# Retention heads summed ungated, and the first gate's rows weighed on VectorE

## The chip, the cores and the metric

The kernel runs on one core of one Trainium2 chip. The time is the device time of one execution in microseconds; smaller is better. The core's engines named below are PE (TensorE, matrix products), DVE (VectorE), ACT (ScalarE), POOL (GpSimd) and SP (SyncE, which here does nothing but issue transfers). The kernel before has three timed runs: 1186.47, 1186.53 and 1189.27 us, so a median of 1186.53 us.

## The reference, cut to what matters

The model is a two-layer diffusion transformer on 256 latent tokens `x` and 256 context tokens `ctx`, each of width 1024, in fp32. Layer 1 mixes tokens by retention (four heads, 256-wide queries and keys, 512-wide values), layer 2 by neighbourhood attention; each layer ends in an MLP with 4096 hidden units. Shifts, scales and gates come from a conditioning vector, through a 1024 x 6144 matrix per layer, once for the latent and once for the context tokens.

```python
for i in range(DEPTH):
    mod = (silu_c @ ada_w[i] + ada_b[i])[:, None, :]
    mod_c = silu_cc @ ada_w[i] + ada_b[i]
    sh1, sc1, g1, sh2, sc2, g2 = jnp.split(mod, 6, axis=-1)
    sh1c, sc1c, g1c, sh2c, sc2c, g2c = jnp.split(mod_c, 6, axis=-1)
    h = x * (1.0 + sc1) + sh1
    hc = ctx * (1.0 + sc1c) + sh1c
    ...                                   # y, yc: the mixer's outputs
    x = layer_norm(DN_ALPHA * x + g1 * y, ln_g[i, 0], ln_b[i, 0])
    h = x * (1.0 + sc2) + sh2
    x = layer_norm(DN_ALPHA * x + g2 * sq_relu_mlp(h, mlp_w1[i], mlp_w2[i]), ...)
    ...                                   # the same for ctx in layer 1
# retention, end of the mixer: heads side by side, then one product
on = on.transpose(0, 2, 1, 3).reshape(b, o.shape[2], v_w)
return (on * jax.nn.silu(g)) @ w_o
```

So the retention's output y is a sum over four heads of a (512-wide) product with that head's rows of `w_o`. The gate `g1` multiplies this sum column by column, and `DN_ALPHA * x` is added to it before the LayerNorm.

## The kernel before, in words

**Products.** Every large product is made of three passes (`mm3`): each operand is split into a rounded high part and the rest, and hi·hi, hi·lo and lo·hi are added in PSUM. Weights come in pieces of 512 KB: SP issues the load into one of four `raw` buffers, ACT casts it to `hi`, and DVE subtracts to make `lo`. The transposed, modulated input (`hTh`, `hTl`) of all 512 tokens stays in SBUF. `R[t]`, t = 0 to 3, holds the residual of the 128-token tile t (two of `x`, two of `ctx`).

**Retention heads.** The loop `for h in range(RH)` does four heads. In each, PE makes queries and keys (tiles `pq`, rotated by DVE and ACT), values (`pv`, evacuated to `vh`, `vl`), the scores (`pS`, which DVE masks with `strips` into `sm` and splits into `sh`, `sl`), the silu gates of tiles 0 and 1 (`pg`), the heads' outputs (`po`, one bank per tile), the gates of tiles 2 and 3, and the output product `pw` with eight 128 x 512 blocks (four tiles, two halves). DVE normalises each `po` as soon as it is done (`bn_stats` into `bs`, `bn_aggr` into `mv`, then `on`, with a `rstd` worked out on POOL), and POOL multiplies it with the silu gate into `gs`. PE transposes `gs` (`pT`) between the products of the gates of tiles 2 and 3 and, for tiles 2 and 3, between the first `pw` blocks; ACT and DVE split that into `oh` and `ol`, the left operand of `pw`.

**The residual.** In the first head ACT multiplies `R` by `ALPHA`. In every head `tok` hands each `pw` block to `accumulate`: DVE makes `acc = pw * G1`, and POOL adds it into `R` (in the fourth head DVE adds two of them itself). `G1` is the gate `g1` broadcast over the partitions, 2 x 512 KB.

**The background stream.** The rest of the conditioning work is a generator `bg_stream`; each `bg()` in the code takes one step of it: it loads one 512 KB chunk of `ada_w` (tile `rawa`, out of the same four `raw` buffers) ahead, and weighs the chunk loaded before. A "part" is eight chunks: part (layer, w, 2) is the gate of block w, parts 0 and 1 its shift and scale. The first part, (0, 0, 2), which is `g1`, goes through PE (`on_pe`): `ada_mm` multiplies each chunk in four 128 x 256 matmuls with 32 columns into `pada`, `ada_row` adds the bias, the row is written out to DRAM (`grow`), and `first_gate` loads it back as `G1`, from the POOL queue, in the first head. The other three layer-1 parts are weighed on DVE (`weigh`): each 128 x 1024 chunk in four instructions over 128 x 512, for latent and context, into two accumulators that lie in the `strips` tile (buffers 118 and 119 below). After four chunks a transposing reduction brings each accumulator into `red`, and one small matmul (`ada_columns` or `ada_gate`) folds that over the partitions. `bg_until(39)` in the fourth head ends these four parts. The later parts, of layer 2, run in the MLP.

**What sets the order.** Each engine works its own queue in order. A scheduler builds these queues ahead of time from the code; it also moves instructions across the order of the code (the masks and reductions of a stretch can trade places), except for those that the code pins with `dve.on` or `act.on`. Transfers issued by SP stand in one queue as well: a load that has to wait for a buffer, or for a row to be written, holds all that is behind it.

**Lines.** All instructions of engines are recorded at a helper's line (L84), so the profile tells them apart by tile names. In the code: `ada_mm` L440, `ada_row` L453, `ada_gate` L488, `weigh` L521, `bg_stream` L535, `load_gate` L616, `accumulate` L756, `proj_T` L1021, `first_gate` L1040, the head loop L1045, the two `act.mul` L1056, `tok` L1196, `bg_until(39)` L1209.

Of the kernel before, what the change touches and what calls it, by code (L numbers as in the profile page):

```python
# [10 lines left out]
F32 = mybir.dt.float32  # L11
F32R = mybir.dt.float32r
AF = mybir.ActivationFunctionType
ALU = mybir.AluOpType
# [90 lines left out]
def kernel(  # L105
# [323 lines left out]

    def ada_bias(l, offs, nb):  # L430
        brow = scr("brow")
        ab = ada_b[l]
        for i in range(2):
            sp.dma_start(
                out=brow[64 * i : 64 * i + 64, :nb],
                in_=bass.AP(ab.tensor, ab.offset + offs[i], [[nb, 2], [0, 32], [1, nb]]),
            )
        return brow

    def ada_mm(pr, k, nb, rhs):  # L440

        lhsT = cT[:, k, :, :].rearrange("p a t -> p (a t)")
        for j in range(4):
            pe.matmul(
                pr[32 * j : 32 * j + 32, 0:nb],
                lhsT=lhsT,
                rhs=rhs(j),
                start=(k == 0),
                stop=(k == KC - 1),
                tile_position=(0, 32 * j),  # L450
            )

    def ada_row(pr, brow, nb, p0=0, p1=P, row=None):  # L453
        if row is None:
            row = smp.tile([P, 256], F32, tag="row", name=nm("row"), bufs=1)
        dve.tensor_add(out=row[p0:p1, :nb], in0=pr[p0:p1, 0:nb], in1=brow[p0:p1, :nb])
        return row

    def folded(red, acc, t, c0, n):
# [48 lines left out]

    def on_pe(l, w, part):
        return (l, w, part) == (0, 0, 2)  # L510

    def bg_load(l, w, part, offs, n):

        if l == 1 or w == 0:
# [20 lines left out]
    def bg_stream():  # L535
# [3 lines left out]
        for l, w, part in (  # L539
            [(0, 0, 2), (0, 1, 0), (0, 1, 1), (0, 1, 2)]  # L540
            + [(1, 0, 0), (1, 0, 1), (1, 0, 2), (1, 1, 0), (1, 1, 1), (1, 1, 2)]
        ):
            sh, sc, g = 3 * w * D, (3 * w + 1) * D, (3 * w + 2) * D
            offs = (sh + 512 * part, sc + 512 * part) if part < 2 else (g, g + 512)
            for n in range(KC):
                plan.append((l, w, part, offs, n))
        nxt = bg_load(*plan[0])
        yield
        for step, (l, w, part, offs, n) in enumerate(plan):
# [4 lines left out]
            nt = 2 if l == 0 or (w == 0 and part < 2) else 1  # L554
            if on_pe(l, w, part):
                if n == 0:
                    pr = bank("pada")
                if n == KC - 2:
                    brow = ada_bias(l, offs, 256)
                ada_mm(pr, n, 256, lambda j: raw[:, j // 2, (j % 2) * 256 : (j % 2 + 1) * 256])  # L560
                if n == KC - 1:
                    row = ada_row(pr, brow, 256)
                    for t in range(2):
                        pool.dma_start(
                            out=grow[l, w][t].rearrange("(j c) -> j c", j=4), in_=row[t:P:32, :]
                        )
                yield
                continue
# [33 lines left out]

    bg_max = [39]

# [415 lines left out]

    def proj_T(th, tl, first=False):  # L1021
        pb = [bank("pq") for _ in range(2)]
        for u in range(2):
            ((wh, wl),) = take(1)
            for dc in range(2):
                for kk in range(4):
                    k = 4 * u + kk
                    mm3(pb[dc][:], (wh[:, kk, tsl(dc)], wl[:, kk, tsl(dc)]), hs(k, 0, NT), k == 0, k == KC - 1)
            if first:
                bg(2)  # L1030
        rotate(pb, th, tl)
# [5 lines left out]

    G1s = [None]

    def first_gate():  # L1040

        if G1s[0] is None and bg_done[0] >= 9:
            G1s[0] = load_gate(0, 0, eng=nc.gpsimd)

    for h in range(RH):  # L1045
        last = h == RH - 1
        if h == 0:
# [29 lines left out]
        gs = slot(S_GS, [P, 4, DV], F32, "gs")  # L1077
        gu = take(4)

        def gates(ts, between=()):  # L1080

            pgs = [bank("pg") for _ in ts]
            for k in range(KC):
                wh, wl = gu[k // 2]
                for t, pg in zip(ts, pgs):
                    mm3(pg[:], hs(k, t * P, (t + 1) * P), (wh[:, k % 2, :], wl[:, k % 2, :]), k == 0, k == KC - 1)
                if h == 0 and k == 3 and len(ts) == 1:
                    bg(2)
                    first_gate()
                if k in between:  # L1090
                    between[k]()
            return pgs

        def gate(t):
            return gates((t,))[0]

# [32 lines left out]
        if h == 0:  # L1129
# [3 lines left out]
            bg()  # L1133
            first_gate()
            pg = gate(1)
            act.activation(out=gs[:, 1, :], in_=pg[:], func=AF.Silu)
        else:
            S = masked_scores()
            for t in range(2):
                pg = gate(t)  # L1140
                act.activation(out=gs[:, t, :], in_=pg[:], func=AF.Silu)
                bg()
        ons = []
        for t in range(4):
# [14 lines left out]
            if t < 2:  # L1159
                pool.tensor_mul(out=gs[:, t, :], in0=on, in1=gs[:, t, :])  # L1160
            if h == 0 and t == 0:
                bg_until(9)
                first_gate()
                bg()
# [20 lines left out]
        bg_until(9)  # L1185
        first_gate()
        G1 = G1s[0]

# [7 lines left out]
        def tok(t, half, us):  # L1196
            accumulate(tok_mm(t, half, us), t, half, G1)

# [9 lines left out]
        else:  # L1208
            bg_until(39)  # L1209
            wus = take(4)  # L1210
# [101 lines left out]
    for hf in range(2):  # L1312
# [9 lines left out]
        if hf == 0:  # L1322
# [34 lines left out]
            outside()  # L1357
        bg_max[0] = 87
        for fp in range(len(hid), 8):
# [18 lines left out]
        for half in range(2):  # L1378
# [23 lines left out]
            bg_until(87)  # L1402
            held = take(4)
# [845 lines left out]
```

## Time and profile before

| | |
|---|---|
| median of the timed runs | 1186.53 us (1186.47 to 1189.27) |
| the profiled execution's own time | 1188.31 us |
| its span | 1186.5 us |
| mean granted clock of TensorE | 0.999 |
| first head, from the second key product to the first `po` | about 60 to 92 us |
| second head | 134.5 to 236.2 us |
| third head | 236.2 to 337.9 us |
| fourth head up to its last product | 337.9 to about 441.6 us |

The profiled execution is 1.78 us longer than the median, and 1.81 us of its time lie outside its span. Spans and starts below are counted in it, in microseconds from the start of the span. In a row of the timeline the first number is the start, the second the busy time of the group, then engine, line, operation, `out<-in`, partitions times elements, and the count; a bracket at the end gives the idle time of the engine just ahead and what ended it. PE's matmuls overlap by their pipeline, so what one costs is read from the distance between starts. A chunk of matmuls `x8` in these records is four matmuls of the order (each of these narrow fp32 matmuls is recorded twice).

### The profile page before, as it was taken

The numbers are of one execution on the slowest core, as the hardware profiler recorded it, in microseconds if no ns is written. First come the engines' busy times: TensorE is split into PE (matmuls) and PEld (weight loads), VectorE is DVE, ScalarE is ACT, GpSimd is POOL, SyncE is SP. The second block draws the span as 40 slices with busy tenths as digits, with TensorE's granted clock in tenths as the row PEclk, the third lists the DMA queues.
The fourth block names the chain that finished last, engine by engine and source line by source line (L and its number), as shares of the span: only waits on it lengthen the run. The fifth ranks groups of instructions, "written<-read, shape, count | busy, mean of one in ns | idle before, by whom it ended". The sixth has DMA issues, their size and how long they took to land.

```text
span 1186.5 us, 17867 instructions
## 1 busy us (share of the span) xinstructions
PE 1176.7 (99%) x6884; PEld 990.9 (84%) x6884; DVE 832.8 (70%) x1304; ACT 480.9 (41%) x813; POOL 248.9 (21%) x389
## 2 busy tenths in 40 slices
PE   9999999999999999999999999999999999999997
PEld 7778888888888889888888888889888878999886
DVE  3876975886688487757876675668467588876446
ACT  3652222322223246441212333137466666665341
POOL 0104301310330141780202000223344430000001
PEclk9999999999999999999999999999999999999999
DMA  9964441444254216756566665637244434765660
GB/s 276 273 234 161 142 158 56 143 130 137 89 160 160 77 55 209 203 112 215 177 193 211 200 213 185 206 108 215 69 143 125 118 122 152 224 201 185 227 212 36
DMA packets 138041, 193.16 MB, mean 163 GB/s; under 512 B 9772, under 2 KB 81108, under 8 KB 137956
## 3 DMA queue, kind: packets, MB, share of 16 engines
q1 hardware_dynamic: 129572, 179.02, 47.3%
q0 software_dynamic: 7232, 10.44, 3.9%
q10 hardware_dynamic: 1152, 2.56, 0.7%
q8 instruction: 54, 0.88, 0.3%
q14 instruction: 31, 0.25, 0.1%
HBM read 187.15 MB, written 5.75 MB: 163 GB/s over the span
## 4 chain that ended last, share of the span: by engine, by line
PE 96%; ACT 1%; DVE 1%; issue 1%; DMA 0%; POOL 0%; DVEq 0%; ACTq 0%
PE p L84 44%; PE pq L84 8%; PE pg L84 7%; PE pv L84 7%; PE pw L84 7%; PE pn L84 5%; PE pnv L84 4%; PE po L84 3%; PE pada L84 2%; PE pnw L84 1%; PE pS L84 1%; PE ppt L84 1%; PE pqk L84 1%; PE pt L84 1%; PE pav L84 1%; PE p1t L84 1%
## 5 line engine op out<-in xcount | busy, mean ns | idle before, releaser
L84 ACT CAST hi<-raw 128x1024 fp32r<-128x1024 f32 (+2 forms) x228 | 232.7, 1032 | 325.0 <-PE p L84 151.3
L84 DVE TENSOR_TENSOR lo<-raw,hi 128x1024 fp32r<-128x1024 f32 (+2 forms) x228 | 280.3, 1240 | 101.8 <-ACT hi L84 101.0
L84 PE MATMUL p<-hi,hid 128*128 128x512 f32 (+1 forms) x832 | 241.8, 374 | 0.0
L84 PEld LDWEIGHTS p<-hi,hid 128*128 128x128 f32 x832 | 152.1, 188 | 27.7
L84 PE MATMUL p<-hTh,lo 128*128 128x256 f32 (+1 forms) x512 | 166.9, 329 | 0.0
L84 PE MATMUL p<-hTl,hi 128*128 128x256 f32 (+1 forms) x512 | 166.9, 329 | 0.0
L84 PE MATMUL p<-hTh,hi 128*128 128x256 f32 (+1 forms) x512 | 164.0, 330 | 0.0
L84 PE MATMUL p<-lo,hid 128*128 128x512 f32 (+1 forms) x416 | 155.3, 373 | 0.0
L84 DVE SCALAR_TENSOR_TENSOR acc<-rawa,scol,acc 128x1024 f32<-128x1024 f32 x56 | 74.7, 1344 | 63.1 <-DMA rawa<-in_ada_w_dram 62.9
L84 POOL TENSOR_TENSOR R<-R,acc 128x512 f32<-128x512 f32 x40 | 62.2, 1565 | 212.3 <-DVE acc L84 212.2
L84 PEld LDWEIGHTS p<-hTl,hi 128*128 128x128 f32 x512 | 96.4, 188 | 8.7
L84 PEld LDWEIGHTS p<-hTh,lo 128*128 128x128 f32 x512 | 96.3, 188 | 8.8
L84 PEld LDWEIGHTS p<-hTh,hi 128*128 128x128 f32 x512 | 95.1, 190 | 8.7
L84 PEld LDWEIGHTS p<-lo,hid 128*128 128x128 f32 x416 | 78.4, 188 | 13.6
L84 ACT CAST hid<-r 128x256 fp32r<-128x256 f32 (+1 forms) x64 | 31.9, 500 | 103.4 <-DVE r L84 103.3
L84 DVE SCALAR_TENSOR_TENSOR strips<-rawa,scol,strips 128x512 f32<-128x512 f32 x84 | 66.4, 847 | 0.0
L84 POOL TENSOR_TENSOR rstd<-rstd,misc 128x1 f32<-128x1 f32 x28 | 19.2, 686 | 215.5 <-DVE rstd L84 214.3
L84 ACT ACTIVATE s<-s,mn 128x512 f32<-128x512 f32 x64 | 45.5, 712 | 26.2 <-DVE mn L84 26.1
L84 PE MATMUL pg<-hi,hTh 128*128 128x512 f32 x128 | 51.1, 399 | 0.0
L84 PE MATMUL pw<-hi,oh 128*128 128x512 f32 x128 | 50.9, 398 | 0.0
L84 PE MATMUL pg<-lo,hTh 128*128 128x512 f32 x128 | 50.0, 391 | 0.0
L84 PE MATMUL pw<-hi,ol 128*128 128x512 f32 x128 | 50.0, 390 | 0.0
(238 smaller groups left out, 2277.1 us busy)
## 6 DMA issues: line engine op xcount, KB each, us to landing
raw<-in_mlp_w_dram SPq DMA_DIRECT2D x128, 512.0 KB, 4.2
rawa<-in_ada_w_dram SPq DMA_DIRECT2D x80, 512.0 KB, 4.3
raw<-in_ret_w_in_dram SPq DMA_DIRECT2D x42, 512.0 KB, 3.6
raw<-in_nat_w_in_dram SPq DMA_DIRECT2D x24, 512.0 KB, 3.9
rawq<-in_ada_w_dram SPq DMA_DIRECT2D x16, 512.0 KB, 5.8
raw<-in_ret_w_o_dram SPq DMA_DIRECT2D x16, 512.0 KB, 4.4
bias<-rpb_rows POOLq DMA_DIRECT2D x32, 128.0 KB, 2.9
raw<-in_nat_w_o_dram SPq DMA_DIRECT2D x8, 512.0 KB, 4.1
```

The source lines that it names most:

```text
L84: r = f(*args, **kwargs)
```

## The change

Four things change.

1. The gate `g1` no longer goes through PE. All four layer-1 parts (`EARLY`) are weighed on DVE, so eight more chunks are weighed, and `g1` is folded by one 32 x 64 matmul in the second head (`ada_gate`), which also loads the bias and writes the two rows from the POOL queue. `ada_bias`, `ada_mm` and `ada_row` go. The stream has 41 steps in the retention where it had 39, and 89 in all ahead of the second layer where it had 87; the steps stand at other places: about 7, 13, 13 and 8 in the four heads, where there were 14, 10, 10 and 6.
2. The outputs of the heads are summed without the gate: ACT copies the first head's eight `pw` blocks into `R`, and in the second and third heads DVE adds `pw` to `R`. The `acc` of these heads and POOL's additions go, and so do the two multiplications by `ALPHA` on ACT.
3. `residual_in(t)` puts the residual in, in the fourth head's code: SP loads `x` or `ctx` again in eight blocks of 256 KB (`xin`, scratch buffers), DVE multiplies `R` by `G1` in place and adds `ALPHA * xin`, in two instructions per block. The fourth head's own output is still gated by `accumulate`.
4. `G1` is loaded by SP in the code of the third head (`load_gate` at h == 2), not by POOL in the first.

```diff
+    EARLY = (0, 0, 2), (0, 1, 0), (0, 1, 1), (0, 1, 2)
...
-            if on_pe(l, w, part):
-                if n == 0:
-                    pr = bank("pada")
-                if n == KC - 2:
-                    brow = ada_bias(l, offs, 256)
-                ada_mm(pr, n, 256, lambda j: raw[:, j // 2, (j % 2) * 256 : (j % 2 + 1) * 256])
-                if n == KC - 1:
-                    row = ada_row(pr, brow, 256)
...
-            if l == 0:
+            if (l, w, part) in EARLY:
                 dve.on = True
...
-    bg_max = [39]
+    bg_max = [41]
...
+    def residual_in(t):
+
+        for half in range(2):
+            sl = slice(half * 512, (half + 1) * 512)
+            xin = scr("xin")
+            sp.dma_start(out=xin[:], in_=(x, ctx_in)[t // 2][0][tsl(t % 2), sl])
+            dve.tensor_mul(out=R[t][:, sl], in0=R[t][:, sl], in1=G1[:, t // 2, sl])
+            dve.scalar_tensor_tensor(
+                out=R[t][:, sl], in0=xin[:], scalar=ALPHA, in1=R[t][:, sl], op0=ALU.mult, op1=ALU.add
+            )
...
-            act.on = True
-            for a in range(2):
-                act.mul(out=RR[a][:], in_=RR[a][:], mul=ALPHA)
-            act.on = False
-            proj_T(qkh[:, 2:4], qkl[:, 2:4], True)
+            proj_T(qkh[:, 2:4], qkl[:, 2:4])
...
+            if h == 2:
+                G1 = load_gate(0, 0, eng=nc.sync)
+            if last:
+                residual_in(0)
             proj_T(qkh[:, 0:2], qkl[:, 0:2])
+            if last:
+                residual_in(1)
+            else:
+                bg()
             proj_T(qkh[:, 2:4], qkl[:, 2:4])
...
+                if last and u == 1:
+                    residual_in(2)
                 bg()
...
+        if last:
+            between[1] = lambda: residual_in(3)
...
         def tok(t, half, us):
-            accumulate(tok_mm(t, half, us), t, half, G1)
+            ps = tok_mm(t, half, us)
+            o = R[t][:, half * 512 : (half + 1) * 512]
+            if h == 0:
+                act.copy(out=o, in_=ps[:])
+            else:
+                dve.tensor_add(out=o, in0=ps[:], in1=o)
...
-            bg_until(39)
+            bg_until(41)
...
-        bg_max[0] = 87
+        bg_max[0] = 89
```

In the fourth head `tok` is not used; its blocks go to `accumulate` as before. The engines' queues change as follows at the places that matter later. Operations are in PE's or DVE's own order, with the number of the buffer behind the name.

PE, first head, the gate product of the second tile. The kernel before:

```order
L84 MATMUL pg_990<-lo_757,hTh 128x512
L84 MATMUL pg_990<-hi_756,hTl 128x512
L84 MATMUL pada_828<-rawa_984,cT 32x256 x4
L84 MATMUL pada_828<-rawa_1003,cT 32x256 x4
L84 MATMUL pg_990<-hi_796,hTh 128x512
L84 MATMUL pg_990<-lo_797,hTh 128x512
L84 MATMUL pg_990<-hi_796,hTl 128x512
```

The changed kernel:

```order
L84 MATMUL pg_958<-lo_757,hTh 128x512
L84 MATMUL pg_958<-hi_756,hTl 128x512
L84 MATMUL pg_958<-hi_794,hTh 128x512
L84 MATMUL pg_958<-lo_795,hTh 128x512
L84 MATMUL pg_958<-hi_794,hTl 128x512
```

Two of the eight chunks stood there, each in four matmuls; nothing stands in their place on PE.

DVE, fourth head, from the last masks of the scores to the evacuation of the first `po`. The kernel before:

```order
L84 TENSOR_TENSOR sm_3350<-pS_3343,strips_119 128x512
L84 TENSOR_TENSOR sl_3309<-sm_3339,sh_3308 128x512
L84 TENSOR_REDUCE red_2624<-strips_118 128x16
L84 TENSOR_TENSOR sl_3309<-sm_3350,sh_3308 128x512
L84 TENSOR_REDUCE red_2624<-strips_119 128x16
L84 BN_STATS bs_3421<-po_3408 128x6
```

The changed kernel, where the four rows of weighing a chunk stand for each of three chunks:

```order
L84 TENSOR_TENSOR sl_3270<-sm_3311,sh_3269 128x512
L84 SCALAR_TENSOR_TENSOR strips_118<-rawa_3248,scol,strips_118 128x512
...
L84 SCALAR_TENSOR_TENSOR strips_118<-rawa_3328,scol,strips_118 128x512
...
L84 SCALAR_TENSOR_TENSOR strips_118<-rawa_3347,scol,strips_118 128x512
L84 SCALAR_TENSOR_TENSOR strips_119<-rawa_3347,scol,strips_119 128x512
L84 TENSOR_REDUCE red_2877<-strips_118 128x16
L84 TENSOR_REDUCE red_2877<-strips_119 128x16
L84 BN_STATS bs_3398<-po_3385 128x6
```

Twelve weighing instructions now stand between the last score and the first `po`, where there were none.

DVE, the end of the third head, its first two `pw` blocks. The kernel before:

```order
L84 TENSOR_TENSOR lo_2798<-raw_2795,hi_2797 128x1024
L84 TENSOR_TENSOR acc_2814<-pw_2801,G_1022 128x512
L84 TENSOR_TENSOR ol_2706<-pT_2817,oh_2705 128x4x128
L84 TENSOR_TENSOR acc_2837<-pw_2824,G_1022 128x512
L84 TENSOR_TENSOR ol_2706<-pT_2840,oh_2705 128x4x128
```

The changed kernel:

```order
L84 TENSOR_TENSOR lo_2748<-raw_2745,hi_2747 128x1024
L84 TENSOR_TENSOR R_104<-pw_2751,R_104 128x512
L84 TENSOR_TENSOR R_104<-R_104,G_2118 128x512
L84 TENSOR_TENSOR ol_2656<-pT_2765,oh_2655 128x4x128
L84 SCALAR_TENSOR_TENSOR R_104<-xin_2918,R_104 128x512
L84 TENSOR_TENSOR R_104<-pw_2772,R_104 128x512
L84 TENSOR_TENSOR R_104<-R_104,G_2118 128x512
L84 TENSOR_TENSOR ol_2656<-pT_2786,oh_2655 128x4x128
```

The residual of the first token tile is put in here already, so three more instructions, one of them on an `xin` load, stand ahead of the second `ol`, the operand that PE needs next.

SP, the same place: the loads that go out near the end of the third head. The kernel before:

```order
L84 DMA raw_2795<-in_ret_w_in_dram 128x4x256
L84 DMA rawa_2847<-in_ada_w_dram 128x2x512
L84 DMA rawa_2885<-in_ada_w_dram 128x2x512
L84 DMA raw_2891<-in_ret_w_in_dram 128x4x256
L84 DMA raw_2897<-in_ret_w_in_dram 128x4x256
```

The changed kernel:

```order
L84 DMA raw_2745<-in_ret_w_in_dram 128x4x256
L84 DMA rawa_2793<-in_ada_w_dram 128x2x512
L84 DMA raw_2829<-in_ret_w_in_dram 128x4x256
L84 DMA xin_2918<-in_x_dram 128x512
L84 DMA xin_2922<-in_x_dram 128x512
L84 DMA raw_2835<-in_ret_w_in_dram 128x4x256
```

The first two `xin` loads stand behind the weights that take the second buffer freed.

More of the change, by code (lines that the diff above doesn't have):

```diff
@@ L428, in ada_load @@
         return raw
[L430 to L457, printed above, removed]
     def folded(red, acc, t, c0, n):
@@ L507, in ada_gate @@
             )
-    def on_pe(l, w, part):
-        return (l, w, part) == (0, 0, 2)
+    EARLY = (0, 0, 2), (0, 1, 0), (0, 1, 1), (0, 1, 2)
     def bg_load(l, w, part, offs, n):
-        if l == 1 or w == 0:
+        if (l, w, part) not in EARLY:
             return ada_load(l, n, offs)
@@ L554, in bg_stream @@
             nt = 2 if l == 0 or (w == 0 and part < 2) else 1
-            if on_pe(l, w, part):
-                if n == 0:
-                    pr = bank("pada")
-                if n == KC - 2:
-                    brow = ada_bias(l, offs, 256)
-                ada_mm(pr, n, 256, lambda j: raw[:, j // 2, (j % 2) * 256 : (j % 2 + 1) * 256])
-                if n == KC - 1:
-                    row = ada_row(pr, brow, 256)
[L563 to L568, printed above, removed]
             if n == 0:
                 red = smp.tile([P, 2, 32], F32, tag="red", name=nm("red"), bufs=2)
-            if l == 0:
+            if (l, w, part) in EARLY:
                 dve.on = True
@@ L1019, in rotate, with proj_T @@
             act.on = False
-    def proj_T(th, tl, first=False):
+    def proj_T(th, tl):
         pb = [bank("pq") for _ in range(2)]
@@ L1078 @@
         gu = take(4)
+        if h == 0:
+            bg()
         def gates(ts, between=()):
@@ L1092, in gates, with gate @@
             return pgs
-        def gate(t):
-            return gates((t,))[0]
+        def gate(t, between=()):
+            return gates((t,), between)[0]
         def masked_scores():
@@ L1133 @@
             bg()
-            first_gate()
             pg = gate(1)
@@ L1139 @@
             for t in range(2):
-                pg = gate(t)
+                pg = gate(t, {} if t else {3: bg})
                 act.activation(out=gs[:, t, :], in_=pg[:], func=AF.Silu)
@@ L1160 @@
                 pool.tensor_mul(out=gs[:, t, :], in0=on, in1=gs[:, t, :])
-            if h == 0 and t == 0:
-                bg_until(9)
-                first_gate()
+            if t == 0:
                 bg()
@@ L1401 @@
                 continue
-            bg_until(87)
+            bg_until(89)
             held = take(4)
```

15 lines of the change are left out of this document (2 added, 13 removed).

## The prediction

> **What bounds the kernel now.** First the page: busy times, then the chain that ended last.
>
> ```profile
> PE 1176.7 (99%) x6884; PEld 990.9 (84%) x6884; DVE 832.8 (70%) x1304; ACT 480.9 (41%) x813; POOL 248.9 (21%) x389
> PE 96%; ACT 1%; DVE 1%; issue 1%; DMA 0%; POOL 0%; DVEq 0%; ACTq 0%
> ```
>
> PE is busy 1176.7 of 1186.5 us, and 96% of the chain is its own. So work taken from PE shortens the program, as long as nobody is late for PE. That has to be read stage by stage: busy time and count of PE, PEld, DVE, ACT and POOL, then the clock and DMA's share, for the first head from its key product to the first `po`, for heads two and three, for the fourth up to its `pw`, and for its end.
>
> ```profile
> 59.90:91.70 31.80, 31.80 (x187) 22.81 (x186) 22.43 (x45) 15.25 (x24) 1.02 (x2) 1.00 0.70 238
> 134.50:236.20 101.70, 101.70 (x470) 84.17 (x469) 76.80 (x114) 28.32 (x40) 20.37 (x21) 1.00 0.39 125
> 236.20:337.90 101.70, 101.70 (x470) 84.17 (x469) 76.79 (x114) 28.32 (x40) 21.70 (x24) 1.00 0.39 124
> 337.90:416.60 78.70, 78.70 (x359) 65.10 (x357) 55.36 (x88) 22.45 (x34) 9.21 (x14) 1.00 0.40 128
> 416.60:441.60 25.00, 24.94 (x122) 20.42 (x121) 19.60 (x39) 11.35 (x20) 13.08 (x13) 1.00 0.14 44
> ```
>
> PE never waits in the first four; the clock is full. DVE has 25 us of 101.7 free in a head, ACT and POOL over 70. The question is therefore how many PE microseconds go, and whether the work put on DVE stays within its holes.
>
> **The change part by part.**
>
> *Off PE: the gate's eight chunks.* In the first head they stand at six places between large products, four alone and two in pairs. I read their price from the starts around them. The last rows, from the fourth head, give the plain step.
>
> ```profile
> 59.91 0.47 PE L84 MATMUL pq<-hTh,hi 128*128 128x512 f32 x1
> 65.25 0.39 PE L84 MATMUL pq<-hTh,lo 128*128 128x512 f32 x1
> 65.57 0.64 PE L84 MATMUL pada<-rawa,cT 128*32 128x256 f32 x8
> 66.47 0.39 PE L84 MATMUL pq<-hTl,hi 128*128 128x512 f32 x1
> 71.49 0.39 PE L84 MATMUL pq<-hTh,lo 128*128 128x512 f32 x1
> 71.81 1.07 PE L84 MATMUL pada<-rawa,cT 128*32 128x256 f32 x16
> 73.15 0.40 PE L84 MATMUL pg<-lo,hTh 128*128 128x512 f32 x1
> 91.69 0.39 PE L84 MATMUL po<-vh,sh 128*128 128x512 f32 x1
> 381.29 0.28 PE L84 MATMUL pS<-qkh 128*128 128x256 f32 x1
> 385.47 0.39 PE L84 MATMUL pg<-hi,hTh 128*128 128x512 f32 x1
> 391.82 0.39 PE L84 MATMUL pg<-lo,hTh 128*128 128x512 f32 x1
> ```
>
> From 385.47 to 391.82 there are 28 steps, so a 512-wide matmul costs 0.227 us. Around a single chunk two large matmuls take 66.47 - 65.25 = 1.22 us instead of 0.45: 0.77 us for the chunk. Around a pair it is 73.15 - 71.49 = 1.66: 1.21 us. That makes 4 x 0.77 + 2 x 1.21 = 5.5 us. Another way: from 59.91 to 91.69 are 31.78 us, in which stand 96 large matmuls (48 of the key product, 48 of two gate tiles; 21.8 us) and the scores, which take 385.47 - 381.29 = 4.18 us in the fourth head; 5.8 us are left. The least that can be meant is the chunks' own busy time, 4 x 0.64 + 2 x 1.07 = 4.7 us. I take 5.6, nearest to the two ways that hold the gaps as well; ends 4.7 and 5.8.
>
> *On PE: one fold.* The gate of the second block is folded today in the fourth head, by just such a 32 x 64 product between large ones.
>
> ```profile
> 416.10 0.39 PE L84 MATMUL pg<-hi,hTl 128*128 128x512 f32 x1
> 416.98 0.39 PE L84 MATMUL pw<-lo,oh 128*128 128x512 f32 x1
> ```
>
> 0.88 us instead of 0.45: 0.4 us, once more now, in the second head. Ends 0.2 (one plain step) and 0.6 (the least price of a single chunk above). Net of PE: 5.6 - 0.4 = 5.2 us less, between 4.1 and 5.6.
>
> *On DVE: the weighing.* Eight more chunks and four more reductions. A chunk is one group of four, measured beside POOL's additions and without them; the third row is what POOL did beside the first.
>
> ```profile
> 335.36 4.42 DVE L84 SCALAR_TENSOR_TENSOR strips<-rawa,scol,strips 128x512 f32<-128x512 f32 x4
> 372.88 2.73 DVE L84 SCALAR_TENSOR_TENSOR strips<-rawa,scol,strips 128x512 f32<-128x512 f32 x4
> 334.91 2.99 POOL L84 TENSOR_TENSOR R<-R,acc 128x512 f32<-128x512 f32 x2 [3.69 <-DVE acc L84]
> 340.31 1.28 DVE L84 TRANSPOSE_TENSOR_REDUCE red<-strips 128x16 f32<-128x512 f32 x2
> 399.27 0.70 DVE L84 BATCH_NORM_STATS2 bs<-po 128x6 f32<-128x512 f32 x1 [9.74 <-PE po L84]
> ```
>
> Alone a chunk takes 2.73 us; beside two POOL additions 4.42, 1.69 more. The Trainium skill ("SBUF — State Buffer", Who interferes with whom) gives a cause: a VectorE instruction with two SBUF inputs and a GpSimd instruction reading SBUF lock each other out for the whole instruction. The trace agrees that they disturb each other, with 1.69 us for two additions; by the full lock it would be up to 2.99, a chunk 5.72, and taking these additions away would free more of DVE. The sum below would be the same by both, since POOL's additions go; the room around it is taken by the row.
>
> The eight chunks are 22 to 35 us in three heads, with 25 us free in each. The additions of POOL go (24 in the first three heads), so the low price is the nearer. The tight place is the stretch before the first `po`: DVE idles 9.74 us there in the fourth head. Now it has three chunks and two reductions: 3 x 2.73 + 1.28 = 9.5 us, which just fits; at the high price 14.5 us, 4.8 too much. DVE's first `po` may then start late, and what is late next is `gs`, which POOL makes and PE transposes:
>
> ```profile
> 400.27 0.22 POOL L84 TENSOR_SCALAR rstd<-mv 128x1 f32<-128x1 f32 x1 [55.82 <-DVE mv L84]
> 402.14 1.28 POOL L84 TENSOR_TENSOR gs<-on,gs 128x512 f32<-128x512 f32 x1 [0.99 <-DVE on L84]
> 404.30 0.81 DVE L84 TENSOR_SCALAR on<-po,mv,rstd 128x512 f32<-128x512 f32 x1 [1.39 <-POOL rstd L84]
> 411.31 0.60 PE L84 MATMUL pT<-cst,gs 128*128 128x128 f32 x4
> ```
>
> `gs` is done at 403.42, and PE wants it at 411.31. That is 7.9 us of cover for this tile, but behind it DVE's queue holds the `lo` and `ol` of the output product. Of 4.8 us late, waits like the 1.39 us ahead of `on`, in four tiles, can give back some 3.3 at most. POOL had stood idle for 55.82 us before its first `rstd`, so nothing is there to raise the price to the high one: no wait of PE in my sum, and 0 to 1.5 us a head for the range.
>
> *Head sums.* Eight gated `acc` of the first head become eight ACT copies, on an engine with over 70 us free a head; in heads two and three a DVE addition takes the place of an `acc`, one for one, both with one PSUM input. POOL's additions and ACT's two multiplications go; neither is on the chain. Worth nothing either way: PE waits for none of it in the first four windows, so there is neither a gain nor, with that room, a loss.
>
> *The residual.* Sixteen DVE instructions more, at 0.7 us each (0.68 is the 512-wide `acc` below) 11 us, spread over the end of the third head and the fourth. The tightest place is the first `pw` blocks of the third head, with three of them ahead of the second `ol` and one `xin` load to wait for:
>
> ```profile
> 311.26 3.55 SPq L84 DMA_DIRECT2D rawa<-in_ada_w_dram  x2
> R<-in_x_dram SPq DMA_DIRECT2D x8, 128.0 KB, 6.5
> 318.86 0.68 DVE L84 TENSOR_TENSOR acc<-pw,G 128x512 f32<-128x512 f32 x1
> 321.86 0.40 PE L84 MATMUL pw<-hi,ol 128*128 128x512 f32 x1
> 322.21 0.69 DVE L84 TENSOR_TENSOR ol<-pT,oh 128x512 fp32r<-128x512 f32 x1 [0.36 <-ACT oh L84]
> 324.62 0.39 PE L84 MATMUL pw<-hi,ol 128*128 128x512 f32 x1
> ```
>
> The second of SP's pair goes out at 311.26 + 3.55 = 314.8 us, and the first `xin` now stands right behind its like; with the 6.5 us that such a load of `x` took at the start it lands at 321.3. DVE comes to it after the sum, the gate and the first `ol`, 318.86 + 3 x 0.68 = 320.9. So: `xin` until 321.3, its own 0.7, sum 0.7, gate 0.7, `ol` 0.7, ends 324.1, against 324.62 on PE. It fits by half a microsecond; the `ol` before it, at 320.9, fits by one. Sum: nothing; range 0 to 1 us. The eight loads are 2 MB, with DMA at 0.39 to 0.40.
>
> *The end of the fourth head.* Two `xin` instructions more on the way into the LayerNorm:
>
> ```profile
> 414.45 1.23 DVE L84 TENSOR_TENSOR lo<-raw,hi 128x1024 fp32r<-128x1024 f32 x1 [1.19 <-ACT hi L84]
> 418.15 2.69 DVE L84 TENSOR_TENSOR lo<-raw,hi 128x1024 fp32r<-128x1024 f32 x1 [1.16 <-ACT hi L84]
> 422.92 0.69 DVE L84 TENSOR_TENSOR acc<-pw,G 128x512 f32<-128x512 f32 x1 [0.75 <-PE pw L84]
> ```
>
> DVE waits 1.19 + 1.16 + 0.75 = 3.1 us here; 2 x 0.7 = 1.4 us fit. Past 422.92 a late DVE would hold PE, which waits for the normalised rows next.
>
> *The gate's load.* Today POOL loads `G1` in the first head; now SP does, behind two tiny writes from POOL's queue. SP's weights queue behind this wait. Bounds: nothing, or what SP's four `raw` buffers do not cover; I take nothing, and a gain is excluded where PE never waits. The Trainium skill (same page, The "DVE blocks DMA" trap) says that a two-port VectorE operation starves descriptors on POOL's queue, about 620 ns becoming 3100; by that the three tiny transfers would hold SP's queue some 2.5 us longer each, an estimate from that page; no run here shows it, and the weights ahead in four buffers would still cover one.
>
> **Sum:** -5.6 + 0.4 = -5.2 us. Against the profiled execution's 1188.31 that is 1183.1; against the median, which is 1.78 lower, 1181.3 us.
>
> **The rivals.**
>
> *Part of the gain is lost (A).* DVE pays the high price in the gate stretch: 4.8 us late, 1.5 us of PE wait in each of three heads, with 1 us at the end of the third: 1181.3 + 5.5 = 1186.8, no change. For it: 9.5 of 9.74 us are filled. Against it: 7.9 us of cover, and POOL's 55.82 us of idle time there.
>
> *Slower: the `xin` loads are late (B).* DVE stands at `xin`, with `lo` and `ol` behind it, and PE waits for these. The loads stand in SP's queue between weights that wait for buffers. If one is held for a whole turn of a buffer, SP's 3.55 us between two issues, and lands 3.55 us later, the third head loses 3.55 - 0.5 = 3.05 us. The fourth has three more such pairs: 4 x 3.05 = 12.2 us, 1193.5. It is slower by over 0.3% (3.6 us, about what can be told from no change) from 8.8 us on, that is from 2.2 us of PE wait at each place. Against it: in the fourth head DVE has 78.7 - 55.36 = 23 us of holes, and the loads wait for scratch buffers that POOL, now emptier, frees.
>
> *It does not do what it says (C).* The matmuls on 32 columns lie under the weight loads of the large ones, and only their gaps go: 2 us, 1184.5. The steps of 1.22 and 1.66 us speak against it.
>
> **How the numbers follow.** Forecast 0.60 (1180.9 to 1182.8, from net 5.6 less 0 to 1.5 us lost, about), A 0.21, B 0.14, C 0.05. Faster by over 0.3% means under 1183.0: the forecast, and the milder third of A, 0.67. Slower means over 1190.1: most of B, 0.12. The same: 0.21. The range reaches from 1180.0 (net 5.6 and a little of the scatter of the runs) to 1187.2, past A's and C's times, and leaves out B and little else.
>
> **What would show it.** The stretch from the key product to the first `po` of the first head at 26.0 to 26.5 us instead of 31.8, with PE still busy throughout; no wait of PE for `ol`, `pT` or weights in the heads; DVE's idle time before the fourth head's first `bs` down from 9.74 to about 0; POOL under 10 us in heads two and three. A wait of PE in the third head's first `pw` blocks, or DVE idle with an `xin` as releaser, would show B; a `bs` that starts long after its `po`, and PE waiting at `pT`, A.

## The result, and the profile after

The changed kernel takes 1180.26 us (median of six runs, 1179.91 to 1182.95), the kernel before 1186.67 us beside it (six runs, 1186.23 to 1189.27). The ratio is 0.9946, with a 95% interval of 0.9935 to 0.9957: faster by 6.4 us, between 5.1 and 7.7. The forecast was 1181.3.

The page after, busy times and chain:

```profile
PE 1167.6 (99%) x6822; PEld 986.4 (84%) x6822; DVE 844.6 (72%) x1349; ACT 480.5 (41%) x819; POOL 212.5 (18%) x364
PE 96%; ACT 1%; DVE 1%; DMA 1%; issue 1%; POOL 0%; DVEq 0%; SPq 0%; ACTq 0%
```

PE is still the bound, with 62 records fewer; DVE has 11.8 us more, POOL 36.4 less. Windows of the changed kernel, with the columns as before: from the key product of the first head to its first `po`, the rest of the first head, the second head, the third, the fourth to its last product.

```profile
60.10:86.19 26.09, 26.09 (x122) 21.80 (x121) 23.76 (x48) 11.64 (x22) 0.00 (x0) 1.00 0.41 139
86.19:128.88 42.69, 42.69 (x197) 35.35 (x196) 28.28 (x41) 15.22 (x21) 9.06 (x13) 1.00 0.42 136
128.88:230.58 101.70, 101.70 (x463) 84.15 (x462) 77.19 (x121) 28.21 (x41) 9.30 (x14) 1.00 0.44 140
230.58:332.70 102.12, 102.12 (x478) 84.24 (x476) 82.99 (x132) 29.02 (x41) 9.84 (x15) 1.00 0.45 140
332.70:436.52 103.82, 103.82 (x479) 85.65 (x478) 84.22 (x143) 33.88 (x53) 19.11 (x23) 1.00 0.43 136
```

The first window is 5.69 us shorter than the 31.78 before. The rest of that head and the second and fourth heads have not moved by 0.02 us, the third is 0.42 longer, and PE waits nowhere in the five. From 60.10 to 436.52 are 376.42 us, where the first trace of before has 441.60 - 59.91 = 381.69: a gain of 5.27.

Two fences on DVE in the changed kernel, the stretch before the fourth head's first `po` and the first `pw` blocks of the third head:

```profile
382.81 8.04 DVE L84 SCALAR_TENSOR_TENSOR strips<-rawa,scol,strips 128x512 f32<-128x512 f32 x12
390.76 1.30 DVE L84 TRANSPOSE_TENSOR_REDUCE red<-strips 128x16 f32<-128x512 f32 x2
394.20 0.70 DVE L84 BATCH_NORM_STATS2 bs<-po 128x6 f32<-128x512 f32 x1 [2.14 <-PE po L84]
```

Three chunks and two reductions take 9.3 us there, the low price, and DVE still has 2.14 us over.

```profile
314.63 0.68 DVE L84 TENSOR_TENSOR ol<-pT,oh 128x512 fp32r<-128x512 f32 x1
315.91 0.69 DVE L84 SCALAR_TENSOR_TENSOR R<-xin,R 128x512 f32<-128x512 f32 x1 [0.60 <-DMA xin<-in_x_dram]
317.85 0.69 DVE L84 TENSOR_TENSOR ol<-pT,oh 128x512 fp32r<-128x512 f32 x1
319.13 0.39 PE L84 MATMUL pw<-hi,ol 128*128 128x512 f32 x1
```

DVE waits 0.60 us for the `xin` load, the only such wait of the eight loads. The second `ol` ends at 318.54, and the PE product that reads it (last row) starts at 319.13.

The spans of the two first traces differ by 8.3 us, more than the medians. Of that 2.8 us lie in the last MLP, where no instruction has changed; the control below takes this up.

### The profile page after: what moved, and what is told of

Same layout as the page of the kernel before. It is cut to its first block, busy times and chain, and to the rows that moved or that the text cites. A ratio compares the mean times of both kernels' runs of the same rounds, so it can differ in the third digit from the quotient of the medians.

```text
span 1178.2 us, 17750 instructions
## 1 busy us (share of the span) xinstructions
PE 1167.6 (99%) x6822; PEld 986.4 (84%) x6822; DVE 844.6 (72%) x1349; ACT 480.5 (41%) x819; POOL 212.5 (18%) x364
## 4 chain that ended last, share of the span: by engine, by line
PE 96%; ACT 1%; DVE 1%; DMA 1%; issue 1%; POOL 0%; DVEq 0%; SPq 0%; ACTq 0%
PE p L84 44%; PE pq L84 8%; PE pv L84 8%; PE pw L84 7%; PE pg L84 7%; PE pn L84 5%; PE pnv L84 4%; PE po L84 3%; PE pnw L84 1%; PE pS L84 1%; PE ppt L84 1%; PE pada L84 1%; PE pqk L84 1%; PE pt L84 1%; PE pav L84 1%; PE p1t L84 1%
## 5 line engine op out<-in xcount | busy, mean ns | idle before, releaser
L84 DVE TENSOR_TENSOR lo<-raw,hi 128x1024 fp32r<-128x1024 f32 (+2 forms) x228 | 273.4, 1213 | 100.2 <-ACT hi L84 100.0
L84 DVE SCALAR_TENSOR_TENSOR strips<-rawa,scol,strips 128x512 f32<-128x512 f32 x112 | 78.5, 762 | 0.0
L84 POOL TENSOR_TENSOR R<-R,acc 128x512 f32<-128x512 f32 x16 | 25.8, 1631 | 169.5 <-DVE acc L84 169.4
L84 PE MATMUL pg<-hi,hTl 128*128 128x512 f32 x128 | 49.9, 390 | 0.0
```

What stands on the lines that cost most here:

```text
L84: r = f(*args, **kwargs)
```

## The experiments

**One chunk instead of eight: what the gate cost PE.** The kernel before, with seven of the eight chunks loaded but not multiplied; the gate lacks them.

```diff
-                start=(k == 0),
-                stop=(k == KC - 1),
+                start=True,
+                stop=True,
...
-                ada_mm(pr, n, 256, lambda j: raw[:, j // 2, (j % 2) * 256 : (j % 2 + 1) * 256])
+                if n == KC - 1:
+                    ada_mm(pr, n, 256, lambda j: raw[:, j // 2, (j % 2) * 256 : (j % 2 + 1) * 256])
```

> The kernel before with seven of the gate's eight chunks not multiplied on PE (so the gate lacks seven eighths of its sum); all loads and all else stay. Theory: 5.6 us of PE time less one chunk's 0.8, 4.8 us, all of it off the end: about 1181.9 us, and 27.0 us from the key product to the first po. Rival (only the gaps go): 2 x 7/8 = 1.75 us less, 1184.9.

The first window of this kernel, and the wait of PE behind it:

```profile
60.10:86.99 26.89, 26.89 (x130) 21.88 (x129) 21.55 (x44) 14.94 (x24) 0.00 (x0) 1.00 0.85 288
108.46 0.50 PE L84 MATMUL pw<-hi,ol 128*128 128x512 f32 x1 [0.85 <-DVE ol L84]
```

1181.24 us (1180.29 to 1182.61) against 1186.37, ratio 0.9955 (0.9938 to 0.9971). The window is 26.89 us where 27.0 were expected, 4.89 less than before and 0.80 more than with no chunk at all. So a chunk alone costs PE 0.8 us, the price read from the starts around it (0.77), and the whole 4.89 us come off this window. That only the gaps go is refuted. The later part of this head lost 1.15 us again, with 0.85 as a wait for `ol`, so the four heads are 3.74 us shorter in this trace. The gate's rows were written no earlier than before (POOL at 90.45 us, 90.68 before), while the first `po` came 4.7 us sooner: POOL's first `rstd`, which stands behind them, made DVE's `on` 2.75 us later against that `po`, and `ol` was still 2.74 us late.

**The second half alone: summing without the gate, residual at the end.** The kernel before with `residual_in`, the new `tok` and without the two `act.mul`, as in the diff of the change; gate and stream as before.

```diff
-            for a in range(2):
-                act.mul(out=RR[a][:], in_=RR[a][:], mul=ALPHA)
...
-            accumulate(tok_mm(t, half, us), t, half, G1)
+            ps = tok_mm(t, half, us)
+            o = R[t][:, half * 512 : (half + 1) * 512]
+            if h == 0:
+                act.copy(out=o, in_=ps[:])
+            else:
+                dve.tensor_add(out=o, in0=ps[:], in1=o)
```

> The kernel before with only the second half of the change: heads summed ungated (ACT copies, DVE additions), residual put in at the fourth head; the gate's rows stay on PE and its load on POOL's queue in the first head. Theory: this half is worth nothing, 1186.7 us within 0.3%, and no PE wait in the heads. Rival: taking POOL's 24 additions away frees DVE and the change's unexplained 1.2 us come from here: 1185.5. Rival of the other sign: the xin loads are late, over 1187.5.

1186.04 us (ten runs, 1185.29 to 1189.28), ratio 0.9999 (0.9987 to 1.0010). The second and third heads of this kernel:

```profile
134.86:236.55 101.69, 101.69 (x469) 84.16 (x468) 71.35 (x112) 28.79 (x41) 8.21 (x12) 1.00 0.39 120
236.55:338.24 101.69, 101.69 (x469) 84.16 (x468) 74.22 (x117) 28.36 (x40) 9.58 (x15) 1.00 0.41 129
```

DVE is 5.4 us less busy in the second head than the 76.80 before, with two instructions fewer; most of it is what POOL's additions had added to its work (weighing instructions of up to 1.79 us before, none over 0.75 here). PE is as long as it was: the four heads take 381.75 us, between the 381.69 and 382.4 of the traces of before. The second half is worth nothing by itself, as the sum had it.

**POOL as the adder again.** The changed kernel with the sums of heads two and three on POOL.

```diff
-                dve.tensor_add(out=o, in0=ps[:], in1=o)
+                sm = scr("hs")
+                act.copy(out=sm[:], in_=ps[:])
+                pool.tensor_add(out=o, in0=o, in1=sm[:])
```

> The changed kernel with the sums of heads two and three put back on POOL (ACT copies each pw block to scratch, POOL adds it to R), so that POOL's additions of 128x512 lie beside DVE's weighing again, in the output products; DVE has sixteen additions fewer. Theory (DVE's holes in that part of a head are wide enough, and PE wants nothing of it): 376.4 us from the key product of the first head to the last product of the retention, as in the changed kernel. Rival: the additions lengthen DVE's work there as they did in the gate stretch, 0.7 us each, 5.6 us a head less the 5.4 us that DVE is spared, and the residual of the third head comes late: 1 to 3 us more.

1180.14 us (1179.78 to 1182.87), ratio 0.9942 (0.9921 to 0.9964), and 436.67 - 60.01 = 376.66 us for the heads. Which engine sums is of no weight for the end. What the second half gives the change is another thing: no head before the third needs `G1` any more, so the gate may be finished late, at 173.6 us, near the middle of the second head, instead of about 90 in the first, and can go through DVE at all. That is read from the code; no run has the first half alone.

**DVE made late before the first `po`.** The changed kernel with 8 unused instructions in the stretch, in heads two to four, and another with 12 (the range below is then 12).

```diff
+            dve.on = True
+            for i in range(8):
+                dm = scr("dm")
+                dve.scalar_tensor_tensor(
+                    out=dm[:], in0=vh[:, 0, :].bitcast(F32), scalar=scol[:, 0, 0:1],
+                    in1=vh[:, 1, :].bitcast(F32), op0=ALU.mult, op1=ALU.add,
+                )
+            dve.on = False
         ons = []
```

> The changed kernel with eight more two-input DVE instructions of 128x512 (their results unused) ahead of the first po's evacuation in heads two to four: 8 x 0.67 = 5.4 us. DVE idles 0.56, 5.00 and 2.14 us there, so it comes late by 4.8, 0.4 and 3.2 us. Theory (7.9 us of cover between gs and its transpose): no PE wait, 1180.3 us. Rival A (only some 3.3 us are given back by the waits on rstd): 1.5 us in the second head, 1181.8.

> The same with twelve: 8.0 us, late by 7.5, 3.0 and 5.9 us. Theory: just within the 7.9 us of cover, 0 to 1 us of PE wait in all, 1180.3 to 1181.3 us. Rival A: 4.2 and 2.6 us in the second and fourth head, 1187.1.

Heads two, three and four with eight:

```profile
128.61:230.31 101.70, 101.70 (x463) 84.16 (x462) 81.65 (x129) 27.80 (x41) 10.20 (x14) 1.00 0.45 141
230.31:333.39 103.08, 102.41 (x477) 84.17 (x476) 87.50 (x140) 29.37 (x41) 10.03 (x15) 1.00 0.44 138
333.39:437.86 104.47, 103.78 (x480) 85.73 (x478) 89.80 (x152) 34.22 (x53) 18.53 (x23) 1.00 0.43 136
```

DVE was less late than expected, since the scheduler put the two reductions behind the first `bs`. Against the 2.92 us from the first `po` to this `bs` in the changed kernel, `bs` came 3.44, 0.22 and 1.87 us late with eight, and 6.09, 2.86 and 4.51 us with twelve. Where PE lost time, first with eight (two rows), then with twelve:

```profile
417.24 0.21 DVE L84 TENSOR_TENSOR gate<-gate 32x64 f32<-32x64 f32 x1 [0.79 <-DMA gate<-in_ada_b_dram]
425.10 1.09 PE L84 MATMUL pt<-cst,xn 128*128 128x128 f32 x8 [0.69 <-ACT xn L84]
203.34 2.25 POOL L84 TENSOR_TENSOR gs<-on,gs 128x512 f32<-128x512 f32 x1 [0.99 <-DVE mv L84]
205.64 0.55 PE L84 MATMUL pT<-cst,gs 128*128 128x128 f32 x3 [0.81 <-POOL gs L84]
426.82 1.09 PE L84 MATMUL pt<-cst,xn 128*128 128x128 f32 x8 [1.44 <-ACT xn L84]
```

With eight the second head is not longer; 3.4 us late, A would have lost only 0.1 us there, so this run does not part the two. The third is 0.96 longer, though hardly late: in this execution the first `xin` load landed 6.7 us after its issue instead of 5.5, `xin` held DVE for 1.79 us instead of 0.60, and PE then waited 0.68 us for the second `ol`. The fourth is 0.65 longer, at the LayerNorm, and the wait there is for a transfer: DVE stood 0.79 us at the bias of the other gate (the second block's), which POOL loads. The same place shows without any lateness: DVE stood 0.39 us at it in the kernel with POOL's sums, and PE 0.31 us at the LayerNorm.

With twelve the three heads take 102.71, 102.79 and 105.21 us, so 1.0, 0.7 and 1.4 longer. In the second head it was the second tile that waited, 0.81 us for a `gs` that took POOL 2.25 us instead of 1.29; in the fourth PE waited 1.44 us at the LayerNorm, and DVE not at all for the bias. The medians of these four-run sets (1183.74 and 1183.42, the changed kernel beside them 1183.09) can't tell such amounts, the stages can. Both theories missed. By 7.9 us of cover nothing should have been lost at 6.1 and 4.5 us late; by A's 3.3 us the second head should have lost 2.8 us with twelve, not 1.0, and only the fourth, 1.2, is near what A gives.

**POOL busy beside DVE in that stretch.** The changed kernel with eight unused POOL additions in heads two to four.

```diff
             S = masked_scores()
+            pool.on = True
+            for i in range(8):
+                dm = scr("dm")
+                pool.tensor_add(out=dm[:], in0=vh[:, 0, :].bitcast(F32), in1=vh[:, 1, :].bitcast(F32))
+            pool.on = False
```

> The changed kernel with eight POOL additions of 128x512 (results unused) beside DVE's work of that stretch in heads two to four. By the row of before, where two POOL additions made a weighed chunk 1.69 us longer, the twelve weighing instructions, 8.04 us now, take up to 8 x 0.85 = 6.8 us more, 14.8; by a full lock (1.29 us an addition) up to 18.3. DVE late by at most 6.2 us: by the theory PE does not wait, 1180.3 us; by rival A up to 2.9 and 1.4 us in heads two and four, 1184.6.

The second head's additions and weighing, and heads two to four of this kernel:

```profile
174.58 13.32 POOL L84 TENSOR_TENSOR dm<-vh 128x512 f32<-128x512 f32 x8
182.18 2.88 DVE L84 TENSOR_TENSOR sl<-sm,sh 128x512 fp32r<-128x512 f32 x2
184.99 10.10 DVE L84 SCALAR_TENSOR_TENSOR strips<-rawa,scol,strips 128x512 f32<-128x512 f32 x12
128.74:234.99 106.25, 103.59 (x464) 85.18 (x462) 83.83 (x121) 28.11 (x41) 23.57 (x22) 0.98 0.44 135
234.99:337.11 102.12, 102.12 (x477) 84.25 (x476) 87.28 (x132) 29.12 (x41) 22.18 (x23) 1.00 0.45 139
337.11:444.54 107.43, 103.77 (x479) 85.74 (x478) 89.62 (x144) 34.31 (x53) 31.90 (x31) 1.00 0.43 132
```

1188.18 us (ten runs), ratio 0.9996 (0.9981 to 1.0011): eight additions a head, whose results nobody uses, take the whole gain away. The additions began earlier than meant, beside the splitting of the scores too (`sl`, 2.88 us instead of 1.45 for two), and DVE's first `bs` came 5.5 us late in the second head. With the 0.56 us that DVE had idled there, its work was 6.1 us longer, 0.76 us for each addition, and POOL's 0.38 (13.32 / 8 = 1.67 instead of 1.29). Only DVE instructions with two inputs in SBUF grew (`lo`, `sl`, the weighing); `sm`, which reads the scores in PSUM, did not (three take 1.34 us, 1.33 in the changed kernel). The Trainium skill ("SBUF — State Buffer", Who interferes with whom) has the second of two such instructions blocked outright; the trace agrees that they disturb each other, but DVE was not held for all of the 8 x 1.29 = 10.3 us, and both engines bear a part, together 1.14 of the 1.29 us that an addition takes alone.

In the fourth head most of the price on PE comes by a transfer: POOL's `gs` took 2.37 us instead of 1.29, the other gate's bias was issued behind it 1.1 us later against the first `po`, and it landed 5.6 us after its issue instead of 3.0. DVE stood 2.69 us at it, and PE waited 3.66 us at the LayerNorm. Why the transfer itself took longer stays open:

```profile
423.94 0.21 DVE L84 TENSOR_TENSOR gate<-gate 32x64 f32<-32x64 f32 x1 [2.69 <-DMA gate<-in_ada_b_dram]
431.79 1.09 PE L84 MATMUL pt<-cst,xn 128*128 128x128 f32 x8 [3.66 <-ACT xn L84]
```

**The `xin` instruction ahead of the first `ol`.** One pair of DVE instructions exchanged in the third head.

```diff
                     tok(t, half, us)
+                    if h == 2 and half == 0 and t == 0:
+                        dve.on = True
+                        residual_in(0, (0,))
+                        dve.on = False
...
             if last:
-                residual_in(0)
+                residual_in(0, (1,))
```

> The changed kernel with one pair of DVE instructions exchanged: in the third head the xin instruction of the first block stands ahead of the first ol, so that ol, and PE behind it, waits for the load. In the changed kernel the load was there at 315.9 us, the ol ran at 314.63, and PE wanted it at 316.4. Theory of B's mechanism (one microsecond late is one microsecond of PE): ol ends at 315.9 + 0.6 + 0.7 = 317.2, PE waits 0.8 to 1.0 us there, and the time rises by as much, 1181.2. Rival: PE finds other work and waits less than 0.3 us.

DVE, PE and the third head's window in this kernel:

```profile
316.60 0.69 DVE L84 SCALAR_TENSOR_TENSOR R<-xin,R 128x512 f32<-128x512 f32 x1 [1.11 <-DMA xin<-in_x_dram]
317.20 0.68 DVE L84 TENSOR_TENSOR ol<-pT,oh 128x512 fp32r<-128x512 f32 x1
317.94 0.50 PE L84 MATMUL pw<-hi,ol 128*128 128x512 f32 x1 [0.64 <-DVE ol L84]
231.35:334.35 103.00, 102.36 (x477) 84.18 (x476) 83.06 (x133) 29.39 (x41) 9.85 (x15) 1.00 0.45 139
```

The head is 0.88 us longer, as expected; 0.64 us are PE's wait itself. The median, 1182.04 us (six runs, 1181.41 to 1184.92), with a ratio of 0.9969 (0.9956 to 0.9981) to before, lies higher than that by itself explains. B's mechanism is real, then: late `xin` is late PE. What it lacked was the lateness.

**Controls.** The kernel before, unchanged, twice, and the changed kernel once more.

> The kernel before, unchanged, for a second trace of it. Between the two traces the spans differ by 8.3 us (1186.5 and 1178.2), the medians by 6.4. By the end of the retention the changed kernel is 5.1 us ahead, as forecast; 2.8 of the other 3.2 us come in the last MLP, whose instructions are the same. If those belong to the one execution that was profiled before, this trace needs about 152 us there instead of 155, and a span of about 1184.5 us. If they belong to the change, it shows 155 again.

> The changed kernel, unchanged, beside these. From the key product of the first head to the last product of the retention 376.4 us again, as in its first trace, and for the last MLP either 159.3 us, as in four of the traces so far, or 162.1, as in both traces of the kernel before, if the longer one can come to any of these kernels.

> The kernel before once more. From the key product to the last product of the retention 381.7 us. In the last MLP 159.3 us if the 162.1 us of its first two traces came by the execution, 162.1 again if they belong to this kernel.

The kernel before took 1189.96 and 1189.33 us in these single executions, the changed kernel 1183.09 where the kernel before took 1189.16 beside it, 2.8 and 2.5 us more than in the first set (ratio 0.9942, 0.9926 to 0.9959). Its heads took 376.49 us again. In both new traces of before they took 382.4 us, 0.7 more than in the first, and a wait of PE in the first head shows why:

```profile
79.44 0.64 PE L84 MATMUL pada<-rawa,cT 128*32 128x256 f32 x8 [0.65 <-DMA rawa<-in_ada_w_dram]
```

This row is of the second trace of before; the third has 0.64 us at the same chunk. The chunk of `ada_w` comes late, and PE, which multiplied it itself, had to wait; the changed kernel has no product there that could.

The last MLP, from its first product to the end of the span, in the first and third traces of before, the changed kernel, and the second-half-alone kernel (in this order):

```profile
1016.68:1178.80 162.12, 162.12 (x1107) 150.55 (x1105) 102.74 (x134) 77.34 (x115) 3.99 (x3) 1.00 0.55 182
1017.69:1179.80 162.11, 162.11 (x1107) 150.57 (x1105) 102.58 (x134) 76.98 (x115) 3.99 (x3) 1.00 0.55 183
1011.16:1170.50 159.34, 159.34 (x1107) 147.80 (x1105) 102.04 (x134) 76.17 (x115) 3.99 (x3) 1.00 0.57 186
1016.84:1176.20 159.36, 159.36 (x1107) 147.83 (x1105) 102.03 (x134) 75.95 (x115) 3.99 (x3) 1.00 0.56 185
```

The same 1107 products take 162.1 us in all three traces of the kernel before and 159.3 in all nine of the others. The expectation that a further trace of before would show the shorter one failed twice. Still it is not put down to the change: in the timed runs of one and the same kernel, the changed one too (1179.91 and 1182.95), executions lie some 3 us apart, and the kernel with the second half alone, with 159.3 in its trace, has the median of the kernel before, 1186.04 to 1186.37. Nor would it fit the timed runs: 5.27 us in the heads and 2.8 here are 8.1 us, beyond the 7.7 that the interval allows. Where these 2.8 us come from stays open. It is left out of the account below.

## Why the prediction was right

*The matmuls off PE*: 5.6 us forecast, 31.78 - 26.09 = 5.69 measured, and 0.80 for one chunk where 0.77 was read. Reading starts around an insertion, instead of the insertion's own busy time (4.7), was the right choice. Not in the sum: the wait of 0.65 us for a late chunk, which two of the four traces have in which PE multiplies all eight chunks (the first trace of before and the second-half-alone kernel do not); where it comes, it belongs to the gain, 5.3 to 6.0 us in the heads by the traces.

*The fold on PE*: 0.4 us forecast in the second head, 0.42 measured in the third. The second head has one fold before and after, only an earlier one now; the added one appears in the third, where two stand instead of one. These are the third head's:

```profile
257.88 0.26 PE L84 MATMUL pada<-red,cst 128*32 128x16 f32 x8
326.93 0.26 PE L84 MATMUL pada<-red,cst 128*32 128x16 f32 x8
```

*The weighing on DVE*: 9.5 us in the tight stretch forecast, 8.04 + 1.30 measured, with no PE wait. The two reductions were counted against the hole by mistake: in the kernel before they stand in the same stretch already, ahead of its 9.74 us of idle time, so only three chunks were added, and 2.14 us are left where the prediction expected about 0. That POOL's idle time there settles the price is confirmed from the other side, by what eight additions do.

*The cover of 7.9 us* is the step that did not hold. It was not needed, since DVE was in time. The prediction took it at one place, between the first tile's `gs` and its transpose; PE's need for the first `ol`, in DVE's queue behind it, is closer. In the second head of the changed kernel that `ol` ends 3.55 us before its product starts, and the kernel before has 3.5 to 4.0 us there in its last three heads (the changed kernel's third and fourth have 1.3 and 3.3). The changed kernel, then the kernel with POOL busy:

```profile
204.11 0.69 DVE L84 TENSOR_TENSOR ol<-pT,oh 128x512 fp32r<-128x512 f32 x1
208.35 0.39 PE L84 MATMUL pw<-hi,ol 128*128 128x512 f32 x1
206.95 3.42 DVE L84 TENSOR_TENSOR lo<-raw,hi 128x1024 fp32r<-128x1024 f32 x2
210.29 0.68 DVE L84 TENSOR_TENSOR ol<-pT,oh 128x512 fp32r<-128x512 f32 x1
```

With POOL busy DVE was 5.5 us late, its two `lo` then lay beside `gs` on POOL and took 3.42 us instead of 2.46, and PE waited 2.65 us for that `ol` (the head lost 4.55 us, 1.9 of them by a lower clock, below). In the runs with only DVE late the scheduler had put these instructions in another order, and 3.4 us were hidden there. A's price is not derived either: four waits of 1.39 us would give back 5.6 us, not 3.3, and the runs show different amounts by head.

*The residual*: the load forecast to be there at 321.3 on the old clock of the trace, 315.8 on the new (5.5 us earlier), was there at 315.9; the second `ol` was to fit by half a microsecond and fitted by 0.59. Part of this is luck:

```profile
310.31 1.28 SPq L84 DMA_DIRECT2D xin<-in_x_dram  x2
```

The load went out 1.0 us later than forecast (309.3 on the new clock) and was 5.5 us under way instead of 6.5, a time read from loads of half the size. In the other traces of the changed order this load took 4.0 to 6.7 us. DVE idle with `xin` as its releaser, named as a sign of B, was there (0.60 us), and B was not: PE did not wait. *The end of the fourth head*: 103.82 us against 103.83, so the two instructions fit. *Head sums and the gate's load*: nothing, by the second half alone and the second head's unchanged 101.70 us.

*The size*: 6.4 us against 5.2, and the interval from 5.1 holds both; the measured 1180.26 us lies only 0.3 us above the lower end of the range. The heads explain 5.3 to 6.0; for the rest no run shows a cause.

## What to carry to other kernels

On an engine that is busy 99% of the time, a small matmul group between large ones costs far more than its share of the arithmetic, here 0.8 us for four with together half the outputs of one large product, whose step is 0.227 us: read it from the starts around it, and ask whether another engine can do it. Making a result needed later is what lets such work move; the restructuring that does so may be worth nothing by itself and should be judged together with what it allows. Where moved work fills a hole to within 2 us, look at what could make it longer, and at the whole queue behind, not at the slack of one consumer.

## What was not expected of the hardware

In the kernel with POOL busy, a pause of PE of 2.65 us in the second head cost 4.55 us, since the clock was low behind it. Two rows of PE, a window with this pause and the one behind it, and two windows with a longer pause in the fourth head (the granted clock is the third number from the right):

```profile
211.02 0.50 PE L84 MATMUL pw<-hi,ol 128*128 128x512 f32 x1 [2.65 <-DVE ol L84]
212.09 0.63 PE L84 MATMUL pw<-hi,ol 128*128 128x512 f32 x1
208.08:211.49 3.41, 0.76 (x4) 0.42 (x3) 3.41 (x4) 0.47 (x1) 3.41 (x2) 1.00 0.52 160
211.49:214.90 3.41, 3.41 (x10) 2.61 (x9) 2.82 (x3) 1.05 (x1) 0.01 (x1) 0.50 0.78 216
426.53:429.94 3.41, 1.60 (x8) 0.98 (x6) 3.34 (x7) 0.00 (x0) 0.55 (x2) 1.00 0.00 0
429.94:433.35 3.41, 1.56 (x11) 1.47 (x12) 3.27 (x7) 1.61 (x3) 1.54 (x2) 1.00 0.00 0
```

The clock is 0.50 for 3.41 us, then full again, and PE's busy time in that head is 103.59 us instead of 101.70. A pause of 3.66 us in the fourth head of the same execution had no such consequence; pauses up to 1.44 us in the other kernels had none either. The Trainium skill ("TensorE: Matmul & The Clock Gate", Part 1: The HAM clock gate) lets the clock fall after an idle window of about 3.4 us in a window that runs freely; the longer pause that cost nothing and the shorter one that did show that length alone does not decide. The stretches of full clock in the traces are whole multiples of 3.413 us (204.80 us ahead of this fall, 60 of them; 1177.60 us, 345 of them, in the first trace of before). In steps of this length, as in the windows above, the short pause lies in one step, in which PE was busy for only 0.76 us, and the long one is divided between two, with 1.60 and 1.56 us. That would explain both, but with a single fall of the clock in the midst of a kernel it is not shown. A PE wait of some microseconds can thus cost almost twice itself, which B's price left out.
